# Attention values of the next pair of heads projected beside a pair's first head, values kept per head

## The chip, the core and the metric

The kernel runs on one core of a Trainium2 chip. The metric is the device time of one execution in microseconds (us). Before the change it is 2232.55 us, the median of three runs (2230.82 to 2233.64). The five engines are named as in the profile: PE (TensorE: matmuls; PEld is its weight load), DVE (VectorE), ACT (ScalarE), POOL (GpSimd) and SP (SyncE, whose queue issues the DMAs of the weights).

## What is computed

Two layers of a hybrid block over 256 latent tokens and 256 context tokens, width 1024. The change touches two of the three branches of the token mixing, and of these only how the values are projected:

```python
aq, ak, av, gu, gv, hq, hff, hfb, hi, hg, gates = split_cols(h @ w_in)
...
vals = jnp.concatenate([av.reshape(B, T, ATT_HEADS, ATT_DV), vc], axis=1)
y_att = att_out(diff_attention(q, keys, vals, lam))      # 8 heads of 128 value columns
...
iv = hi.reshape(B, T, HG_HEADS, HG_DV)                   # HGRN2, 8 heads of 128 value columns
_, o_f = hgrn2_scan(k_f, iv, lf_f, s_f, q=qh)
```

Each head needs its own projections: HGRN's forget gates (`w_hff`, both directions), its query and output gate (`w_hqg`), attention's query and key (`w_aqk`). The value matrices, `w_hi` of HGRN and `w_av` of attention, come in blocks of 256 columns, so one block serves a pair of heads (0 and 1, 2 and 3, and so on). All eight heads of a layer work alike; layer 1 computes outputs for the 256 latent tokens only (NQ = 256 instead of 512).

## The kernel before

Each f32 operand is held as two parts, so that a product takes three matmuls (`mm3`, L121 to L123). `load_w` brings a weight block in through SP (two DMAs of 512 KB into `wr`), ACT copies it to `wh` (L111) and DVE subtracts for `wl` (L112). The loads run ahead of the work with high priority; there are three `wr`, four `wh` and four `wl` buffers, a block takes two of each.

The heads stage of a layer goes head by head. While head h's own work runs (`hg_head`: decay levels, scores, state, output; `att_head`: scores, softmax, transposes, values), the projections of head h+1 run on PE. Both are written as Python generators, and `weave` interleaves them: the projections are the main stream, cut into units (one `yield` each: 12 matmuls 512 columns wide, or 24 matmuls 256 wide), and the steps of `hg_head` (13) and `att_head` (11 in layer 0, 7 in layer 1) are spread evenly over 0.92 of the units that `units(h)` counts. PE's instructions stay in the order in which this code issues them. The other engines' order is made by the framework's scheduler when the program is built. All engines work in order.

`project(h)` issues, in layer 0, four units each for `w_hff`, `w_hqg` and `w_aqk` (in layer 1 four, two and three). For an even h it also issues four units for `w_hi` ahead of these and four for `w_av` behind them (`v_proj`, each block 4 units of 24 matmuls). So the weave of an even head (which projects an odd one) has 12 units in layer 0 and 9 in layer 1, and that of an odd head 20 and 17. Head 7 is woven with the next stage's projections (`tail_proj`). `v_proj` copies its two PSUM results to one SBUF tile `v` of 4 x 256 values on ACT (L405); three such tiles rotate.

Three groups of PE instructions carry the argument. Those at L602 (scores of attention) open a head. Those at L626 multiply values by the softmax weights. Those at L321 (`column_sums`) are sums over squares: ACT squares a result (L316), ACT copies its high part (L192), DVE subtracts for the low part (L193, tile `sqs`), then PE sums. L321 runs for attention's norm near the end of a head (just before L534), and for HGRN's norm as its last step (after L543 and L546). The levels' exponents are differences made on DVE (L441, tile `E`) which the scheduler also issues ahead for the next head.

Of the kernel before, what the change touches and what calls it, by code (L numbers as in the profile page):

```python
# [17 lines left out]
P = 128  # L18
# [3 lines left out]
HEADS = 8  # L22
# [25 lines left out]
def trunk(ctx: ExitStack, tc: tile.TileContext, A, out):  # L48
    nc = tc.nc
# [348 lines left out]
    def v_proj(get, src, X, out, name, w=None):  # L398
        if w is None:
            w = load_w(src)  # L400
        v = get("v", [P, 4, 256])
        for tt in range(2):
            ps = PB([P, 2, 256])
            yield from tm_steps(w, X, (2 * tt, 2 * tt + 1), ps)
            nc.scalar.copy(out=v[:, 2 * tt:2 * tt + 2, :], in_=ps)  # L405
        out[name] = v
# [529 lines left out]
    for l in range(DEPTH):  # L936
# [5 lines left out]
        def putter(b, h):  # L942
            return lambda t: nc.sync.dma_start(out=ysp[b, h], in_=t)
# [22 lines left out]
        tc.keep_in_program_order(pre)  # L966
        with pool("heads", lk=2, qg=1, qk=1, v=3, w=2, sq=2, sqs=2 if l else 1, wt=2, sc=1, E=6 if l else 4, K=2, p=2) as get, ExitStack() as even, \
                tc.issue_after(pre.ins):
# [3 lines left out]

            def project(h, out, pss=None):
                if pss is not None:
                    yield from hg_proj(gets[h % 2], l, h, Xh, NQ, out, pss)
                if h % 2 == 0:
                    yield from v_proj(get, A["w_hi"][l, h // 2], Xh, out, "vh", whi if h == 0 else None)
                if pss is None:
                    yield from hg_proj(gets[h % 2], l, h, Xh, NQ, out)
                yield from att_proj(gets[h % 2], l, h, Xh, rope, NQ, out)  # L980
                if h % 2 == 0:
                    yield from v_proj(get, A["w_av"][l, h // 2], Xh, out, "va")

            def units(h):
                return (12 if l == 0 else 9) + (8 if h % 2 == 0 else 0)

            d = {}
            for _ in project(0, d, first):
                pass
            for h in range(HEADS):  # L990
                j = slice((h % 2) * P, (h % 2 + 1) * P)
                m = [hg_head(get, l, h, d["ls"], d["k"], d["qg"][:, 0, :], d["qg"][:, 1, :], d["vh"][:, :, j], putter(1, h),
                             lbv, (reset, masks), NQ),
                     att_head(get, l, d["qk"], d["va"][:, :, j], putter(0, h), attv[l], NQ)]
                if h + 1 < HEADS:
# [216 lines left out]
```

## Time and profile before

| | us |
|---|---|
| median of three runs | 2232.55 |
| the profiled execution's own time | 2240.42 |
| its span, first to last instruction | 2238.6 |
| heads 0 to 5 of layer 0, of the span | 101.11 to 507.85 |
| heads 0 to 5 of layer 1, of the span | 1452.55 to 1763.08 |

The stages are told apart by PE's first matmul at L602 of each head: the window of head h goes from there to the same matmul of head h+1. Such a window holds the units of head h's weave but for the first one or two, and the first one or two of the next weave. The busy time of an engine is what it worked in the window; the rest is idle. PEclk is the granted clock of TensorE as a share of 2.4 GHz; at 0.50 it is 1.2 GHz.

### The profile page before, as it was taken

The page shows a single profiled execution, that of the slowest core. Times are in us where ns is not written, and L with a number is a line of the kernel's source. Part 1 is how long each engine was busy: PE and PEld are TensorE (multiplying, and loading weights), DVE is VectorE, ACT ScalarE, POOL GpSimd, SP SyncE. Part 2 cuts the span into 40 slices and gives each one's busy share as a digit, 9 for nine tenths or more (in the row PEclk, how much of TensorE's full clock was granted, in tenths as well). Part 3 has the DMA queues.
Part 4 walks back from the last instruction along what each step waited for, and adds up shares of the span by engine and source line. Part 5 has one row for each costly group of instructions (what it writes and reads, how often), then busy time and mean ns, then how long its engine had stood idle before and what let it go on. Part 6 is the DMA issues. An engine that isn't in the chain of part 4 may idle for free. (4 is left out here: it accounts for less than half of the span.)

```text
span 2238.6 us, 32836 instructions
## 1 busy us (share of the span) xinstructions
PE 2136.9 (95%) x12448; PEld 1860.9 (83%) x12448; DVE 1713.4 (77%) x2869; ACT 1155.8 (52%) x1920; POOL 315.7 (14%) x272
## 2 busy tenths in 40 slices
PE   8999999999999998989999998999999989997998
PEld 7888788887888886878887877988888879997997
DVE  6799888989767884358776766898899976567786
ACT  3766665656543223245342334666666655455664
POOL 3332132322200000011000002222221210001000
PEclk9999999999999999999999999999999999998999
DMA  7212212212255754344555653322222336654554
GB/s 283 94 67 73 70 66 76 73 65 66 62 174 193 235 161 112 94 159 136 166 187 182 198 148 105 104 91 90 81 90 86 97 99 218 195 183 142 186 194 138
DMA packets 93488, 293.21 MB, mean 131 GB/s; under 512 B 16017, under 2 KB 20753, under 8 KB 93073
## 3 DMA queue, kind: packets, MB, share of 16 engines
q1 hardware_dynamic: 93042, 290.59, 40.1%
q8 instruction: 98, 1.61, 0.3%
q14 instruction: 60, 0.49, 0.1%
q10 hardware_dynamic: 288, 0.52, 0.1%
HBM read 282.66 MB, written 8.41 MB: 130 GB/s over the span
## 5 line engine op out<-in xcount | busy, mean ns | idle before, releaser
L121 PE MATMUL pm<-X,wh 128*128 128x512 f32 (+1 forms) x2032 | 716.1, 352 | 11.0 <-DVE X L255 6.5
L122 PE MATMUL pm<-X,wh 128*128 128x512 f32 (+1 forms) x2032 | 699.0, 344 | 0.0
L123 PE MATMUL pm<-X,wl 128*128 128x512 f32 (+1 forms) x2032 | 698.8, 344 | 0.0
L112 DVE TENSOR_TENSOR wl<-wr,wh 128x1024 fp32r<-128x1024 f32 (+1 forms) x402 | 496.8, 1242 | 203.5 <-ACT wh L111 198.9
L111 ACT CAST wh<-wr 128x1024 fp32r<-128x1024 f32 x408 | 422.0, 1039 | 310.7 <-PE pm L122 172.2
L121 PEld LDWEIGHTS pm<-X,wh 128*128 128x128 f32 x2032 | 386.8, 190 | 61.2 <-DVE X L255 7.9
L123 PEld LDWEIGHTS pm<-X,wl 128*128 128x128 f32 x2032 | 387.1, 190 | 47.3
L122 PEld LDWEIGHTS pm<-X,wh 128*128 128x128 f32 x2032 | 386.5, 190 | 42.1
L225 DVE SCALAR_TENSOR_TENSOR wj<-wa,scr 128x1024 f32<-128x1024 f32 x128 | 156.4, 1222 | 63.4 <-DMA wa<-in_ada_row 60.4
L447 POOL TENSOR_TENSOR K<-qg,E 128x512 f32<-128x512 f32 (+1 forms) x96 | 132.3, 1380 | 461.9 <-PE ps L507 304.3
L121 PE MATMUL pm<-wl,X 128*128 128x256 f32 (+1 forms) x608 | 188.0, 309 | 0.0
L122 PE MATMUL pm<-wh,X 128*128 128x256 f32 (+1 forms) x608 | 183.7, 302 | 0.0
L123 PE MATMUL pm<-wh,X 128*128 128x256 f32 (+1 forms) x608 | 183.7, 302 | 0.0
L202 POOL TENSOR_TENSOR s<-s,mhalf 128x1 f32<-128x1 f32 x26 | 14.3, 550 | 1078.4 <-DVE s L199 1052.7
L121 PE MATMUL pm<-ys,wh 128*128 128x512 f32 (+1 forms) x384 | 129.9, 338 | 10.6 <-ACT wh L111 7.4
L441 DVE TENSOR_TENSOR E<-lk 128x512 f32<-128x512 f32 (+1 forms) x192 | 124.4, 681 | 9.5 <-PE ps L546 8.1
L123 PE MATMUL pm<-ys,wl 128*128 128x512 f32 (+1 forms) x384 | 129.5, 337 | 0.0
L122 PE MATMUL pm<-ys,wh 128*128 128x512 f32 (+1 forms) x384 | 129.5, 337 | 0.0
L121 PEld LDWEIGHTS pm<-wl,X 128*128 128x128 f32 x608 | 117.7, 194 | 6.5 <-issue 2.2
L122 PEld LDWEIGHTS pm<-wh,X 128*128 128x128 f32 x608 | 117.8, 194 | 4.0
L123 PEld LDWEIGHTS pm<-wh,X 128*128 128x128 f32 x608 | 117.4, 193 | 4.2
L442 ACT ACTIVATE E<-E 128x1024 f32<-128x1024 f32 (+1 forms) x96 | 80.9, 846 | 59.9 <-DVE E L441 58.9
(250 smaller groups left out, 3541.3 us busy)
## 6 DMA issues: line engine op xcount, KB each, us to landing
wr<-in_w_up SPq DMA_DIRECT2D x88, 512.0 KB, 4.4
wa<-in_ada_row SPq DMA_DIRECT2D x80, 512.0 KB, 4.1
wr<-in_w_gate SPq DMA_DIRECT2D x48, 512.0 KB, 4.0
wr<-in_w_dn SPq DMA_DIRECT2D x40, 512.0 KB, 4.1
wr<-in_w_hqg SPq DMA_DIRECT2D x32, 512.0 KB, 3.6
wr<-in_w_hff SPq DMA_DIRECT2D x32, 512.0 KB, 3.6
wr<-in_w_aqk SPq DMA_DIRECT2D x32, 512.0 KB, 3.6
wr<-in_w_hi SPq DMA_DIRECT2D x16, 512.0 KB, 4.0
```

The costliest lines, as they stand in the source:

```text
L111: nc.scalar.copy(out=hi, in_=raw)
L112: eng.tensor_tensor(out=lo, in0=raw, in1=hi.bitcast(F32), op=sub)
L121: nc.tensor.matmul(ps, lhsT=lh, rhs=rl, start=first, stop=False)
L122: nc.tensor.matmul(ps, lhsT=lh, rhs=rh, start=False, stop=False)
L123: nc.tensor.matmul(ps, lhsT=ll, rhs=rh, start=False, stop=last)
L202: nc.gpsimd.tensor_tensor(out=r, in0=r, in1=mhalf, op=ALU.pow)
L225: nc.vector.scalar_tensor_tensor(out=junk, in0=raw, scalar=1.0, in1=scr[:, v, :], op0=mul, op1=mul, accum_out=mod[l][:, m, v:v + 1])
L441: nc.vector.tensor_tensor(out=dst, in0=ref if first else src, in1=src if first else ref, op=sub)
L442: nc.scalar.activation(out=E, in_=E, func=AF.Exp)
L447: nc.gpsimd.tensor_tensor(out=mkap(KQ[:], dims, NQ), in0=mkap(q, dims), in1=mkap(E[:], [[2 * b, np_], [b - NQ, 2], [1, b]], NQ), op=mul)
```

## The change

`v_proj` fills two tiles, one per head, of 4 x 128 values, with two copies of 128 x 256 per PSUM result where there was one of 128 x 512; six such tiles rotate. `w_hi` of the next pair stays where it was (beside the second head of a pair, ahead of its units). `w_av` of the next pair moves from the end of the second head's weave to the end of the first head's. `units` counts four units more in the weave of each head but 6 (and 7), so that weaves 0 to 5 have 16 units each in layer 0 and 13 in layer 1.

```diff
     def v_proj(get, src, X, out, name, w=None):
...
-        v = get("v", [P, 4, 256])
+        v = [get("v", [P, 4, P]) for _ in range(2)]
         for tt in range(2):
             ps = PB([P, 2, 256])
             yield from tm_steps(w, X, (2 * tt, 2 * tt + 1), ps)
-            nc.scalar.copy(out=v[:, 2 * tt:2 * tt + 2, :], in_=ps)
+            for i in range(2):
+                nc.scalar.copy(out=v[i][:, 2 * tt:2 * tt + 2, :], in_=ps[:, :, i * P:(i + 1) * P])
         out[name] = v
...
-        with pool("heads", lk=2, qg=1, qk=1, v=3, w=2, sq=2, ...
+        with pool("heads", lk=2, qg=1, qk=1, v=6, w=2, sq=2, ...
...
                 if h % 2 == 0:
-                    yield from v_proj(get, A["w_hi"][l, h // 2], Xh, out, "vh", whi if h == 0 else None)
+                    yield from v_proj(get, A["w_hi"][l, h // 2], Xh, out, ("vh", h // 2), whi if h == 0 else None)
...
-                if h % 2 == 0:
-                    yield from v_proj(get, A["w_av"][l, h // 2], Xh, out, "va")
+                c = 0 if h == 0 else (h + 1) // 2 if h % 2 and h < HEADS - 1 else None
+                if c is not None:
+                    yield from v_proj(get, A["w_av"][l, c], Xh, out, ("va", c))
 
             def units(h):
-                return (12 if l == 0 else 9) + (8 if h % 2 == 0 else 0)
+                return (12 if l == 0 else 9) + (4 if h < HEADS - 1 else 0)
...
-                j = slice((h % 2) * P, (h % 2 + 1) * P)
-                m = [hg_head(get, l, h, d["ls"], d["k"], d["qg"][:, 0, :], d["qg"][:, 1, :], d["vh"][:, :, j], putter(1, h),
+                vh, va = d["vh", h // 2][h % 2], d["va", h // 2][h % 2]
+                m = [hg_head(get, l, h, d["ls"], d["k"], d["qg"][:, 0, :], d["qg"][:, 1, :], vh, putter(1, h),
                              lbv, (reset, masks), NQ),
-                     att_head(get, l, d["qk"], d["va"][:, :, j], putter(0, h), attv[l], NQ)]
+                     att_head(get, l, d["qk"], va, putter(0, h), attv[l], NQ)]
```

SP's queue in layer 0, from the weights of head 1 on, shows the order in which PE uses the blocks. Before:

```order
L110 DMA wr<-in_w_hff 128x1024 x2
L110 DMA wr<-in_w_hqg 128x1024 x2
L110 DMA wr<-in_w_aqk 128x1024 x2
L110 DMA wr<-in_w_hi 128x1024 x2
L110 DMA wr<-in_w_hff 128x1024 x2
L110 DMA wr<-in_w_hqg 128x1024
L943 DMA ysp<-sq 128x512
L110 DMA wr<-in_w_hqg 128x1024
L110 DMA wr<-in_w_aqk 128x1024
L943 DMA ysp<-sq 128x512
L110 DMA wr<-in_w_aqk 128x1024
L110 DMA wr<-in_w_av 128x1024 x2
```

and now:

```order
L110 DMA wr<-in_w_hff 128x1024 x2
L110 DMA wr<-in_w_hqg 128x1024 x2
L110 DMA wr<-in_w_aqk 128x1024 x2
L110 DMA wr<-in_w_av 128x1024 x2
L110 DMA wr<-in_w_hi 128x1024 x2
L110 DMA wr<-in_w_hff 128x1024 x2
L110 DMA wr<-in_w_hqg 128x1024
L944 DMA ysp<-sq 128x512
L110 DMA wr<-in_w_hqg 128x1024
L110 DMA wr<-in_w_aqk 128x1024
L944 DMA ysp<-sq 128x512
L110 DMA wr<-in_w_aqk 128x1024
```

The block `w_av` of heads 2 and 3 now follows head 1's `w_aqk`, and the two value blocks stand next to each other; behind head 2's `w_aqk` the next head's `w_hff` follows at once.

On DVE, what stands ahead of the low part of HGRN's last sum (L193 on `sq`) near the end of a head in layer 1. Before, at the end of head 2 (projecting head 3):

```order
L424 SCALAR_TENSOR_TENSOR lk<-reset,lk 128x512
L425 SCALAR_TENSOR_TENSOR lk<-reset,lk 128x512
L441 TENSOR_TENSOR E<-lk 128x4x64
L112 TENSOR_TENSOR wl<-wr,wh 128x1024
L428 TENSOR_TENSOR w<-lk 128x256
L441 TENSOR_TENSOR E<-lk 128x4x64
L441 TENSOR_TENSOR E<-lk 128x8x32 x2
L441 TENSOR_TENSOR E<-lk 128x16x16
L445 TENSOR_TENSOR K<-lk,E 128x256
L193 TENSOR_TENSOR sqs<-sq,sqs 128x256
```

and now, at the end of head 3 (projecting head 4, `w_aqk` last, as before at the end of head 2):

```order
L425 SCALAR_TENSOR_TENSOR lk<-reset,lk 128x512
L426 SCALAR_TENSOR_TENSOR lk<-reset,lk 128x512
L112 TENSOR_TENSOR wl<-wr,wh 128x1024
L429 TENSOR_TENSOR w<-lk 128x256
L442 TENSOR_TENSOR E<-lk 128x4x64
L193 TENSOR_TENSOR sqs<-sq,sqs 128x256
L442 TENSOR_TENSOR E<-lk 128x4x64
L193 TENSOR_TENSOR sqs<-w,sqs 128x256
```

Of the next head's level work four instructions more (L441 three times, L445) stood ahead of the sum's operand than now (line numbers behind L405 grow by one).

## Rows read from the trace of the kernel before

**Rows 1.** The page's first section: busy us of each engine, share, instructions.

```profile
PE 2136.9 (95%) x12448; PEld 1860.9 (83%) x12448; DVE 1713.4 (77%) x2869; ACT 1155.8 (52%) x1920; POOL 315.7 (14%) x272
```

**Rows 2.** Windows, layer 0, heads 0 to 5: us, busy of PE, PEld, DVE, ACT, POOL, PEclk, DMA.

```profile
101.11:162.17 61.06, 58.19 (x329) 49.05 (x329) 56.15 (x101) 40.02 (x71) 21.93 (x12) 0.97 0.19 66
162.17:235.41 73.24, 72.90 (x449) 63.66 (x448) 60.93 (x104) 44.66 (x77) 16.69 (x12) 1.00 0.23 76
235.41:299.09 63.68, 58.35 (x329) 48.89 (x329) 60.12 (x103) 38.80 (x70) 19.40 (x12) 0.97 0.20 71
299.09:372.31 73.22, 72.91 (x449) 63.67 (x448) 59.91 (x102) 44.67 (x77) 16.60 (x12) 1.00 0.21 69
372.31:434.63 62.32, 58.26 (x329) 48.92 (x329) 58.19 (x102) 39.36 (x71) 23.14 (x12) 0.97 0.21 72
434.63:507.85 73.22, 72.89 (x448) 63.66 (x448) 60.92 (x104) 44.24 (x77) 16.67 (x12) 1.00 0.21 69
```

**Rows 3.** The same for heads 0 to 5 of layer 1.

```profile
1452.55:1493.44 40.89, 37.78 (x261) 33.39 (x260) 39.03 (x80) 27.20 (x55) 10.96 (x12) 1.00 0.32 109
1493.44:1554.25 60.81, 59.92 (x404) 53.56 (x404) 53.11 (x104) 39.44 (x75) 10.88 (x13) 1.00 0.27 83
1554.25:1598.36 44.11, 40.61 (x263) 36.08 (x262) 40.45 (x83) 28.45 (x58) 11.85 (x12) 0.92 0.27 91
1598.36:1659.27 60.91, 60.02 (x406) 53.70 (x406) 53.31 (x104) 39.02 (x74) 10.49 (x12) 1.00 0.26 83
1659.27:1702.17 42.90, 39.38 (x262) 34.87 (x262) 40.87 (x81) 27.73 (x57) 11.41 (x12) 0.96 0.28 93
1702.17:1763.08 60.91, 60.24 (x405) 53.89 (x404) 53.58 (x105) 39.59 (x76) 11.21 (x12) 1.00 0.27 84
```

**Rows 4.** PE's waits, 101.11 to 507.85: us in total, times, longest.

```profile
PE ps L321 <- DVE sqs L193: 4.9, 5, 1.8
PE ps L626 <- DVE sc L465: 3.1, 2, 1.5
```

**Rows 5.** PE's waits, 1452.55 to 1763.08.

```profile
PE ps L321 <- DVE sqs L193: 7.7, 6, 2.7
PE ps L602 <- POOL qk L585: 1.8, 1, 1.8
```

**Rows 6.** Timeline of PE, end of head 2, layer 0: start, us, instruction, idle before.

```profile
280.47 0.72 PE L321 MATMUL ps<-sqs,onesr 128*128 128x512 f32 x2 [1.81 <-DVE sqs L193]
```

**Rows 7.** Timeline of DVE just ahead of that.

```profile
277.43 2.38 DVE L441 TENSOR_TENSOR E<-lk 128x512 f32<-128x512 f32 x2
279.74 0.68 DVE L193 TENSOR_TENSOR sqs<-sq,sqs 128x512 fp32r<-128x512 f32 x1
```

**Rows 8.** Windows of stretches at the lower clock.

```profile
281.52:284.93 3.41, 3.41 (x13) 2.83 (x12) 3.41 (x7) 2.98 (x6) 2.17 (x3) 0.50 0.19 74
1588.82:1595.65 6.83, 6.08 (x28) 6.11 (x29) 6.83 (x17) 3.24 (x7) 2.08 (x3) 0.50 0.17 56
```

**Rows 9.** Timelines of PE and DVE, end of head 2, layer 1.

```profile
1583.73 0.59 PE L121 MATMUL pm<-X,wh 128*128 128x512 f32 x1
1589.57 0.77 PE L321 MATMUL ps<-sqs,onesr 128*128 128x256 f32 x2 [2.69 <-DVE sqs L193]
1585.72 2.50 DVE L441 TENSOR_TENSOR E<-lk 128x256 f32<-128x256 f32 x4
```

**Rows 10.** Groups by line and form, 101.11 to 507.85: count, busy us, mean ns.

```profile
L405 ACT COPY v<-pm 128x512 f32<-128x512 f32 x13 | 7.5, 580 | 9.4 <-PE pm L123 9.4
L621 ACT COPY wt<-ps 128x256 f32<-128x256 f32 x12 | 4.3, 360 | 1.4 <-PE ps L619 1.3
L112 DVE TENSOR_TENSOR wl<-wr,wh 128x1024 fp32r<-128x1024 f32 x50 | 64.4, 1295 | 13.2 <-ACT wh L111 13.1
```

**Rows 11.** Timeline of PE: first and last of 24 matmuls of a value unit.

```profile
1599.25 0.39 PE L121 MATMUL pm<-wl,X 128*128 128x256 f32 x1
1602.07 0.28 PE L123 MATMUL pm<-wh,X 128*128 128x256 f32 x1
```

More of the change, by code (lines that the diff above doesn't have):

```diff
@@ L966, in trunk @@
         tc.keep_in_program_order(pre)
-        with pool("heads", lk=2, qg=1, qk=1, v=3, w=2, sq=2, sqs=2 if l else 1, wt=2, sc=1, E=6 if l else 4, K=2, p=2) as get, ExitStack() as even, \
+        with pool("heads", lk=2, qg=1, qk=1, v=6, w=2, sq=2, sqs=2 if l else 1, wt=2, sc=1, E=6 if l else 4, K=2, p=2) as get, ExitStack() as even, \
                 tc.issue_after(pre.ins):
```

## The prediction, as put on record

> **What bounds the kernel now.** I read the page first: PE is busy 95% of the span [rows 1], so time can come only from stretches where PE stands idle or runs slowly. Then the windows of the heads stages, one row per head. The reader should compare even rows with odd rows. In layer 0 [rows 2], the windows of the odd heads have no idle PE to speak of (73.24 - 72.90 = 0.34 us, then 0.31 and 0.33) while DVE has 12.3, 13.3 and 12.3 us to spare. The windows of the even heads are the reverse: PE idles 2.87, 5.33 and 4.06 us, and DVE is busy 92 to 94% of the window. Layer 1 [rows 3] reads alike: PE idles 3.11, 3.50 and 3.52 us in even windows and 0.89, 0.89 and 0.67 in odd ones; DVE idles 1.9 to 3.7 us in even, 7.3 to 7.7 in odd windows. So two engines take turns as the bound: an even head, woven with few projections, is held by DVE, an odd head by PE. PE idles 13.2 us in the six windows of layer 0 and 12.6 us in those of layer 1, 25.8 in all.
>
> The lists of PE's waits say who is late: mostly DVE, with the low part of a sum's operand (L193 to L321) and the masked score copy ahead of the values (L465 to L626) [rows 4, 5]. The timeline shows how: at 280.47 PE has waited 1.81 us for L193 [rows 6], and L193 had stood behind 2.38 us of level work (L441) [rows 7]. That L441 belongs to the next head; DVE's order puts it ahead.
>
> Behind some of these gaps the granted clock falls. The window from 281.52 to 284.93 is at 0.50, which is 1.2 GHz, right behind the 1.81 us gap; that from 1588.82 to 1595.65 goes with the 2.69 us gap at 1589.57 [rows 8, 9]. In the twelve windows there are three stretches like the first in layer 0 and, in layer 1, the second and one more of 3.41 us. At half the clock the busy part loses half: 4 x 3.41 / 2 + 6.08 / 2 = 9.9 us. With the idle time that makes 35.7 us within reach.
>
> **The move.** One `w_av` block per pair of heads goes from the odd head's weave to the even head's. A value unit of PE takes 24 matmuls; first to last start is 2.82 us [rows 11], 23 steps of 0.123, so 24 of them are 2.9 us and the block 11.8 us. Nothing is saved by that in itself: PE does the same matmuls. With it go two DMAs on SP's queue, two ACT copies and two DVE subtractions of 1.3 us [rows 10]. They stay in the order of use behind `w_aqk`, no load passes another that is needed sooner, and PE's waits inside these windows are at sums, values and scores, the largest of them in [rows 4, 5], and none is for a weight, so I cost these loads at nothing; the cover is the four units of `w_aqk` ahead of them. If it failed, one wait would be about 1.3 us, one late L112.
>
> What the move does is to level the windows. In layer 0, DVE's busy time over what PE needs (its busy time less the 1.7 us lost to the clock) is 174.5 / 169.7 = 1.03 in even windows and 181.8 / 218.7 = 0.83 in odd ones; levelled, it is 356.3 / 388.4 = 0.92 in both. In layer 1 the six windows give 280.4 us of DVE to 297.9 - 4.7 = 293.2 of PE, 0.96. Now if idle time grew in proportion to that share, levelling would change nothing: 0.92 is the mean of both. The gain rests on the curve being bent: at 0.83 PE idles 0.33 us, and it cannot idle less than zero, at 1.03 it idles 4.1. So I go wait by wait.
>
> *Even heads, layer 0.* Their last two steps are now hidden behind value units, which leave no work on DVE, and two units instead of one stand ahead of HGRN's sum; their middle steps have 16 units in place of 12 over which to spread. I take the odd windows' 0.33 plus 0.3 for attention's sum: 0.63 each, 1.9 for three, against 12.3 now.
>
> *Odd heads, layer 0.* These lose something. Between the values (L626) and attention's sum (L321) they had two units; now they have one, of `w_aqk`, as an even head has today. There the wait is between nothing and the 1.8 us of [rows 6]; all waits at L321 in layer 0 make 4.9 us in five [rows 4], 1.0 each. I take 1.0 and add 0.33, and 0.3 for the scores of the next head, which now follow `w_aqk` more closely: 1.6 each, 4.9 for three, against 1.0 now. Layer 0 goes from 13.2 to 6.8: 6.4 us.
>
> *Even heads, layer 1.* Here the wait is HGRN's sum at the head's end, up to 2.69 us [rows 9]. There the operand stood behind four L441 (2.50 us) and one unit of PE, 3.2 us from 1583.73 to where the gap begins, had to hide it. Now a value unit hides it, with DVE's projection work long done. The following head's scores (1.8 us once [rows 5]) also get four units of cover. I take the odd windows' 0.8: 2.4 for three, against 10.1.
>
> *Odd heads, layer 1.* They inherit `w_aqk` at the end, but DVE's order now has only one L441 of the next head ahead of the sum's operand instead of four and a K product. That takes about 2 of the 2.69 us out. I take 0.8 plus 0.6: 1.4 each, 4.2 against 2.5, with bounds of nothing and 2.7 for the sum. Layer 1 goes from 12.6 to 6.6: 6.0 us.
>
> *Clock.* Of six stretches' worth (four of 3.41 us and one of twice that) I let two remain, since some waits of over 1 us stay in odd windows: 9.9 x 4/6 = 6.6 us back. Bounds: nothing and 9.9.
>
> *The split copy.* A copy of 512 values a partition takes 580 ns, and two of 256 take 2 x 360 = 720 [rows 10]. That is 0.14 us for each of 32 results, 4.5 us of ACT in the whole kernel. ACT is busy 52% [rows 1], and behind these copies nothing of the same unit waits: four PSUM buffers rotate and the values are used a head later. Zero, with 4.5 as the upper bound if every one lay on the path. Six half tiles hold what three whole ones did, and the two that a block fills are the ones that the head before has left.
>
> Heads 6 and 7 and all other stages are left as they are.
>
> Sum: 6.4 + 6.0 + 6.6 = 19.0 us off the profiled execution's own 2240.42, 2221.4. The median of the runs is 7.9 us below that execution, so the same step gives 2232.55 - 19.0 = 2213.5.
>
> The Trainium skill, "Perfetto Trace Analysis", section on optimization strategy, says that a kernel whose most contended engine changes over time may gain by interleaving its regimes; this case's trace agrees so far, with DVE busy 92 to 94% of the even and PE over 99% of the odd windows of layer 0. Its section on the most-contended engine warns, however, that matmul busy time is a poor measure of TensorE and weight-load busy time a better one. By that, the result would be another, which stands below as a rival.
>
> **The rivals.**
>
> *The waits only change places.* The odd windows take over the even ones' waits, since they now end with `w_aqk` and start with the next `w_hff` behind them. For it: one unit of cover at L321, in-order DVE. Against it: value units at their start, and 58 us of DVE in 65 of PE instead of 58 in 57. The idle time stays at 25.8, give or take 3: 2229 to 2236.
>
> *Slower: DVE falls behind in every window.* From the odd head's `w_hff` to the even head's `w_aqk` there are now 24 units in a row that each leave work on DVE; the value block that stood in their middle, in which DVE catches up (its 12 to 13 us of idle time in odd windows of layer 0 [rows 2]), is gone. If DVE stays late all through, each of the twelve windows idles as an even one does now: 6 x 4.09 + 6 x 3.38 = 44.8 us against 25.8, 19 us more, 2251.5. It decides from a mean of 35.7 / 12 = 3.0 us lost per window, clock included. Against it: the share of 0.92 is below 1.
>
> *PE had room all along.* If PE's true load is its weight loads, an even window of layer 0 has 61.06 - 49.05 = 12.0 us free [rows 2], which would swallow the 11.8 us block whole, and each odd window would shrink by that: 6 x 11.8 = 71 us, 2162. Against it: a stream of 512-column matmuls without a wait runs in the odd windows with no idle PE, so the weight loads' gaps are no room. The Trainium skill, "Perfetto Trace Analysis", section on the most-contended engine, is what suggests this reading; the trace speaks against it, with 0.3 us of idle PE at 63.7 us of weight loads in 73.2.
>
> *The change does not do what it says*: the copies hold up the PSUM buffers or the halves wait for one another, and the gain is eaten, 2230 to 2235. The order of SP shows that the block does move.
>
> **How the numbers follow.** Chances: the forecast 0.77, the waits change places 0.12, slower 0.08, room in PE 0.01, not as said 0.02. The forecast's own range: at best every window idles as odd ones do now (6 x 0.33 + 6 x 0.82 = 6.9 us) and no clock is lost, 25.8 - 6.9 + 9.9 = 28.8, or 2203.8; at worst the odd windows' bounds are all met (3 x 0.8 more in layer 0, 3 x 2.1 more in layer 1) and half the clock's gain, 3.3, stays out, 19.0 - 2.4 - 6.3 - 3.3 = 7.0, or 2225.6; with the copies' 4.5, 2230. The range of 2203 to 2232 holds that and about half of the rival whose waits change places. A measurement of this kernel can tell about 0.2%, 4.5 us: faster than 2228.1 is 0.76 of the forecast and the 0.01, 0.77; within it 0.01 + 0.10 + 0.02, so 0.13; slower 0.02 + 0.08 = 0.10.
>
> **What would show it.** Right: the windows of heads 0 to 5 become alike (about 66 us each in layer 0, 50 in layer 1), PE's idle time falls to 1 or 2 us in each, DVE's spare time is 5 to 7 us in each of layer 0, no stretch at 0.50 lies in most of them, L321 waits stay at odd heads only. Wrong: idle time of 3 us or more in odd windows, waits at L121 for L112, a wait at L602 at the start of even heads, or ACT's value copies ending PE's waits. Most likely to be mis-sized: L321 in odd heads and the clock.

## The result and the profile after

The changed kernel takes 2262.28 us, the median of four runs (2256.97 to 2265.09), against 2233.1 for the kernel before in the same comparison: a ratio of 1.013 with an interval of 1.0109 to 1.0151. It is slower by 29 us where 19 us less were forecast. The profiled execution took 2263.59, its span is 2261.8, 23.2 more than that of the kernel before (the profiled execution of before lay 7 us over its median, that of after 1 us). Lines of the changed kernel are numbered one higher than before from L405 on: L602 is L603, L441 is L442, L626 is L627 and so on.

The first section of the page reads much as before [rows 1]: PE is busy 2141.4 us and DVE 1724.7. Then the windows of heads 0 to 5 of layer 0, which answer to [rows 2] (length, then busy time of PE, PEld, DVE, ACT and POOL, PEclk, DMA):

```profile
103.39:175.00 71.61, 67.38 (x414) 58.87 (x414) 61.60 (x103) 42.28 (x76) 15.25 (x12) 0.98 0.24 80
175.00:244.22 69.22, 64.92 (x365) 54.41 (x365) 61.31 (x102) 41.74 (x75) 17.56 (x12) 1.00 0.20 67
244.22:315.89 71.67, 67.48 (x413) 58.80 (x413) 60.13 (x102) 42.27 (x75) 15.31 (x12) 0.98 0.20 68
315.89:385.11 69.22, 64.98 (x366) 54.41 (x366) 61.32 (x102) 41.74 (x75) 17.57 (x12) 1.00 0.20 67
385.11:455.13 70.02, 65.83 (x413) 57.31 (x413) 60.69 (x102) 42.27 (x75) 15.32 (x12) 1.00 0.21 71
455.13:523.17 68.04, 62.30 (x354) 52.15 (x354) 60.21 (x101) 41.74 (x75) 17.55 (x12) 1.00 0.19 63
```

The windows did become alike, 68 to 72 us. PE's own work in the six is as before (392.9 us, 393.5 before). But PE now idles about 4.2 us in each of them (71.61 - 67.38, and so on; 5.7 in the last), 26.9 in all against 13.2, and DVE has 8 to 12 us to spare in every one. An even head idles as much as it did on average, and an odd head, which lost 0.33, idles as much as an even one. Layer 1 answers to [rows 3]:

```profile
1467.26:1518.74 51.48, 48.72 (x357) 44.77 (x356) 47.02 (x91) 33.97 (x67) 9.33 (x12) 1.00 0.32 103
1518.74:1569.34 50.60, 48.62 (x310) 42.46 (x309) 41.24 (x76) 29.29 (x59) 8.97 (x11) 1.00 0.27 89
1569.34:1626.72 57.38, 51.21 (x356) 46.65 (x357) 54.24 (x112) 38.61 (x76) 14.48 (x13) 0.97 0.25 83
1626.72:1677.31 50.59, 48.61 (x310) 42.45 (x309) 40.69 (x76) 29.01 (x58) 8.52 (x11) 1.00 0.26 83
1677.31:1735.47 58.16, 53.22 (x356) 48.79 (x356) 54.38 (x113) 38.09 (x76) 14.11 (x13) 0.91 0.26 83
1735.47:1786.05 50.58, 48.63 (x309) 42.46 (x308) 39.51 (x74) 29.02 (x58) 9.16 (x11) 1.00 0.26 82
```

Here the odd heads (second, fourth, sixth row) take 50.6 us with 2.0 idle, but the even heads 2 and 4 take 57.4 and 58.2 with 6.2 and 4.9 idle, and both lose time to the clock as well (PEclk 0.97 and 0.91). The sum over layer 1 is 19.8 us idle against 12.6.

By the lengths, the twelve windows account for 13.0 + 8.3 = 21.3 of the 23.2 us. PE's waits in layer 0, as in [rows 4] (in total, times, longest):

```profile
PE ps L321 <- DVE sqs L193: 9.5, 6, 2.7
PE ps L508 <- DVE sc L466: 7.2, 6, 1.6
PE ps L528 <- DVE E L520: 4.7, 3, 1.6
```

and in layer 1, as in [rows 5]:

```profile
PE ps L321 <- DVE sqs L193: 14.1, 7, 3.9
PE ps L603 <- ACT p L609: 2.4, 2, 1.2
```

In layer 0 the larger waits come back in each head of a kind, to 0.1 us (at attention's sum 2.69, 2.69 and 2.65 us in the even heads): this is no noise, but the order of the instructions. The largest of an even head stands at attention's sum. Its timeline in head 2 of layer 0 (start, us, engine, instruction, idle before), PE first, then ACT, then DVE:

```profile
295.37 1.19 PE L321 MATMUL ps<-sqs,onesr 128*128 128x512 f32 x2 [2.69 <-DVE sqs L193]
```

```profile
291.24 0.63 ACT L192 CAST sqs<-sq 128x512 fp32r<-128x512 f32 x1
```

```profile
291.15 0.87 DVE L456 TENSOR_TENSOR E<-lk 128x512 f32<-128x512 f32 x1
...
291.93 0.47 DVE L578 STREAM_SHUFFLE sh<-pm 128x256 f32<-128x256 f32 x1
292.27 0.42 DVE L579 TENSOR_TENSOR t<-pm,cos 128x256 f32<-128x256 f32 x1
292.59 1.69 DVE L112 TENSOR_TENSOR wl<-wr,wh 128x1024 fp32r<-128x1024 f32 x1
294.20 0.41 DVE L584 TENSOR_TENSOR t<-t,sh 128x256 f32<-128x256 f32 x1
294.54 0.68 DVE L193 TENSOR_TENSOR sqs<-sq,sqs 128x512 fp32r<-128x512 f32 x1
```

ACT had finished the operand of L193 at 291.87. DVE took L193 up at 294.54, 2.67 us later, without a gap in its own work: it did the rest of a level (L456), the rope (rotation by position) of the next head's keys (L578 to L584) and the low part of a weight block (L112), all of which stand ahead of L193 in its order. PE's whole wait of 2.69 us is that queue of work. DVE's 11.5 us of idle time in this window are elsewhere. Cut into six equal parts, the same window shows where:

```profile
244.22:256.17 11.95, 11.84 (x61) 9.11 (x61) 10.91 (x19) 9.33 (x19) 1.63 (x1) 1.00 0.18 69
256.17:268.11 11.94, 11.94 (x71) 10.23 (x71) 11.94 (x26) 8.41 (x15) 3.00 (x2) 1.00 0.13 45
268.11:280.06 11.95, 10.55 (x60) 8.47 (x59) 11.95 (x19) 5.62 (x12) 1.31 (x1) 1.00 0.27 89
280.06:292.00 11.94, 11.94 (x78) 10.68 (x77) 11.31 (x24) 7.98 (x12) 4.95 (x4) 1.00 0.00 0
292.00:303.94 11.94, 9.26 (x53) 8.58 (x52) 8.30 (x14) 4.61 (x9) 4.41 (x4) 0.86 0.32 111
303.94:315.89 11.95, 11.95 (x99) 11.73 (x98) 5.72 (x7) 6.32 (x10) 0.00 (x0) 1.00 0.31 97
```

DVE is full from 256 to 280 and nearly so to 292, and it is busy for only 5.72 of 11.95 us in the last part, where value units now stand. The heads are levelled against one another; a head is not levelled in itself. That alone does not cost the time, though, as e12 will show: there a head is as uneven, and PE hardly waits.

### The profile page after: what moved, and what is told of

It reads as the page before. It is cut to its first block, busy times and chain, and to the rows that moved or that the text cites. A ratio compares the mean times of both kernels' runs of the same rounds, so it can differ in the third digit from the quotient of the medians.

```text
span 2261.8 us, 32865 instructions
## 1 busy us (share of the span) xinstructions
PE 2141.4 (95%) x12448; PEld 1863.5 (82%) x12448; DVE 1724.7 (76%) x2869; ACT 1158.9 (51%) x1952; POOL 292.3 (13%) x272
## 5 line engine op out<-in xcount | busy, mean ns | idle before, releaser
L112 DVE TENSOR_TENSOR wl<-wr,wh 128x1024 fp32r<-128x1024 f32 (+1 forms) x402 | 501.3, 1253 | 211.1 <-ACT wh L111 206.5
L448 POOL TENSOR_TENSOR K<-qg,E 128x512 f32<-128x512 f32 (+1 forms) x96 | 125.1, 1305 | 474.9 <-PE ps L508 308.7
L442 DVE TENSOR_TENSOR E<-lk 128x512 f32<-128x512 f32 (+1 forms) x192 | 113.6, 623 | 11.5 <-PE ps L547 7.5
L443 ACT ACTIVATE E<-E 128x1024 f32<-128x1024 f32 (+1 forms) x96 | 80.9, 846 | 54.4 <-DVE E L442 53.3
```

Source lines behind the costliest of these rows:

```text
L112: eng.tensor_tensor(out=lo, in0=raw, in1=hi.bitcast(F32), op=sub)
L442: nc.vector.tensor_tensor(out=dst, in0=ref if first else src, in1=src if first else ref, op=sub)
L443: nc.scalar.activation(out=E, in_=E, func=AF.Exp)
L448: nc.gpsimd.tensor_tensor(out=mkap(KQ[:], dims, NQ), in0=mkap(q, dims), in1=mkap(E[:], [[2 * b, np_], [b - NQ, 2], [1, b]], NQ), op=mul)
```

## The experiments

Each kernel was run with the kernel before beside it. In the table, idle is PE's idle time in heads 0 to 5 of a layer, from the first scores matmul of head 0 to that of head 6, and the ratio is to the kernel before in the same comparison. The order of layer 0 before the change was profiled four times, three of them with the split copies (before, e1, e6, e9), and idles 13.2, 15.3, 17.3 and 15.0 us: a difference of less than some 4 us between two rows tells nothing.

| kernel | median us | ratio, interval | idle, layer 0 | idle, layer 1 |
|---|---|---|---|---|
| before | 2232.55 | | 13.2 | 12.6 |
| after | 2262.28 | 1.0130, 1.0109 to 1.0151 | 26.9 | 19.8 |
| e1_split_only | 2234.87 | 1.0010, 0.9993 to 1.0027 | 15.3 | 12.9 |
| e2_av_first | 2267.93 | 1.0162, 1.0147 to 1.0178 | 27.2 | 25.1 |
| e3_sums_on_pool | 2277.94 | 1.0211, 1.0185 to 1.0236 | 30.5 | 19.2 |
| e4_hi_even_av_odd | 2244.33 | 1.0050, 1.0033 to 1.0066 | 25.1 | 11.4 |
| e5_empty_step | 2260.11 | 1.0124, 1.0095 to 1.0153 | 26.2 | 20.0 |
| e6_hybrid | 2224.33 | 0.9970, 0.9944 to 0.9995 | 17.3 | 11.6 |
| e7_e4_empty_step | 2244.78 | 1.0053, 1.0036 to 1.0070 | 25.3 | 5.2 |
| e8_before_empty_step | 2262.06 | 1.0131, 1.0104 to 1.0158 | 29.0 | 14.6 |
| e9_hybrid_empty_l1 | 2230.14 | 0.9983, 0.9964 to 1.0001 | 15.0 | 5.5 |
| e10_rate_100 | 2252.88 | 1.0097, 1.0069 to 1.0125 | 13.2 | 20.9 |
| e11_rate_108 | 2269.09 | 1.0160, 1.0133 to 1.0188 | 32.6 | 20.4 |
| e12_level_rate | 2222.74 | 0.9964, 0.9950 to 0.9977 | 10.8 | 5.1 |
| e13_after_no_lo | 2240.35 | 1.0050, 1.0031 to 1.0068 | 17.7 | 12.9 |
| e14_before_no_lo | 2220.35 | 0.9959, 0.9943 to 0.9974 | 14.0 | 8.5 |
| e15_before_rate_100 | 2262.22 | 1.0133, 1.0111 to 1.0156 | 33.5 | 13.3 |
| e16_rate_096 | 2260.13 | 1.0133, 1.0116 to 1.0150 | 26.0 | 19.1 |

### The copies, and where the value blocks stand

**e1_split_only** keeps the half tiles and the two copies and puts `w_av` back where it was.

```diff
-                c = 0 if h == 0 else (h + 1) // 2 if h % 2 and h < HEADS - 1 else None
-                if c is not None:
-                    yield from v_proj(get, A["w_av"][l, c], Xh, out, ("va", c))
+                if h % 2 == 0:
+                    yield from v_proj(get, A["w_av"][l, h // 2], Xh, out, ("va", h // 2))
...
-                return (12 if l == 0 else 9) + (4 if h < HEADS - 1 else 0)
+                return (12 if l == 0 else 9) + (8 if h % 2 == 0 else 0)
```

> The changed kernel with the w_av block put back at the end of the second head's weave (units 12 and 20, as before); the half tiles and the two copies of 256 stay. Theory A (the 24 units in a row that each leave work on DVE are the cause): the waits of before come back, 2233 us, within 5. Theory B (the split copies or the half tiles cost the time): 2245 to 2262. Theory C (attention's and HGRN's sums wait because their low parts, L193, stand behind other work in DVE's order): as A, 2233, since the old spacing of steps comes back too.

1.001 (0.9993 to 1.0027): the copies cost nothing that can be told, at most 0.3%. The loss is the move's.

**e2_av_first** puts the moved block at the start of the even head's weave, so that value units and units that leave work on DVE alternate in blocks.

```diff
+                if h % 2 and h < HEADS - 1:
+                    yield from v_proj(get, A["w_av"][l, (h + 1) // 2], Xh, out, ("va", (h + 1) // 2))
...
-                c = 0 if h == 0 else (h + 1) // 2 if h % 2 and h < HEADS - 1 else None
-                if c is not None:
-                    yield from v_proj(get, A["w_av"][l, c], Xh, out, ("va", c))
+                if h == 0:
+                    yield from v_proj(get, A["w_av"][l, 0], Xh, out, ("va", 0))
```

> The changed kernel with w_av at the start of the even head's weave instead of at its end: 16 and 13 units a weave as now, but each run of 12 units that leave work on DVE is followed by 4 value units. Theory A: PE's idle time in heads 0 to 5 falls from 46.7 us to 25 or less, 2210 to 2238 us. Theory C (sums one unit behind their values, whatever the order of the blocks): both weaves now end with w_aqk, the L321 waits of 23.6 us stay, 2250 to 2265.

**e4_hi_even_av_odd** ends every head with a value block: `w_hi` of the next pair in even heads, `w_av` in odd ones, 16 and 13 units as in the changed kernel.

```diff
-                if h % 2 == 0:
-                    yield from v_proj(get, A["w_hi"][l, h // 2], Xh, out, ("vh", h // 2), whi if h == 0 else None)
+                if h == 0:
+                    yield from v_proj(get, A["w_hi"][l, 0], Xh, out, ("vh", 0), whi)
...
-                c = 0 if h == 0 else (h + 1) // 2 if h % 2 and h < HEADS - 1 else None
-                if c is not None:
-                    yield from v_proj(get, A["w_av"][l, c], Xh, out, ("va", c))
+                if h % 2 == 0:
+                    yield from v_proj(get, A["w_av"][l, h // 2], Xh, out, ("va", h // 2))
+                elif h < HEADS - 1:
+                    yield from v_proj(get, A["w_hi"][l, (h + 1) // 2], Xh, out, ("vh", (h + 1) // 2))
```

> The changed kernel with w_hi of the next pair at the end of the even head's weave and w_av of the next pair at the end of the odd head's: 16 and 13 units a weave, each run of 12 (9) units followed by 4 value units, and every head ends with value units. Theory A: idle time at 25 us or less, 2205 to 2235 us. Theory C: the L321 waits of even heads as now (2.7 us each in layer 0), odd heads like them, 2250 to 2265 us.

Heads 0 to 5 of layer 0 and of layer 1 as one window each, e2 and then e4:

```profile
104.23:520.32 416.09, 388.85 (x2293) 331.63 (x2292) 367.93 (x612) 250.74 (x450) 100.79 (x72) 1.00 0.21 70
1463.76:1793.71 329.95, 304.83 (x1969) 270.92 (x1969) 277.82 (x539) 198.58 (x393) 60.79 (x71) 0.96 0.25 84
```

```profile
104.18:527.58 423.40, 398.29 (x2317) 341.01 (x2316) 360.75 (x611) 253.39 (x451) 92.77 (x72) 0.98 0.20 68
1471.47:1774.73 303.26, 291.85 (x1993) 260.84 (x1993) 279.65 (x556) 204.01 (x402) 68.43 (x72) 1.00 0.28 92
```

In layer 0 these places of the blocks make no difference to the idle time: 416.09 - 388.85 = 27.2 and 423.40 - 398.29 = 25.1 us, 4.2 to 4.5 per head, as after the change. The waits behind it differ. In e2 every head waits as an odd head of the changed kernel does (1.6 us at L508, 1.5 at L528, 0.7 at L620 and 0.5 at attention's sum), in e4 every head waits 2.65 us at attention's sum. In layer 1 the place matters: with a value block at the end of every head (e4) the windows take 303.3 us, 15.5 less than after the change and 7.3 less than before it, and heads 2 and 4, which took 57 to 58 us, take 50; with one at the start of every head (e2) the six take 330. Both times lie outside the ranges of both theories on record; only e4's waits at attention's sum are as one of them had it. Both kernels break the run of 24 units (18 in layer 1) that each leave work on DVE, so breaking it does not bring the time back, in layer 0 in either kernel and in layer 1 in e2. What helps in layer 1 goes with the block at the end of the odd heads, which the even heads follow, and the traces show the waits that go. After the change PE waits in head 2 for 0.6 and 1.2 us at its scores (L603), with the odd head's `w_aqk` just ahead of them, and 3.9 us at HGRN's last sum (L321, behind L547); in e4 it has none of these.

### One wait taken away

**e3_sums_on_pool** lets POOL make the sums' low parts (L193 of `rms_square`), which DVE took up late.

```diff
-    def split(t, src):
+    def split(t, src, eng=nc.vector):
...
-        nc.vector.tensor_tensor(out=t[:, 1, :], in0=src, in1=t[:, 0, :].bitcast(F32), op=sub)
+        eng.tensor_tensor(out=t[:, 1, :], in0=src, in1=t[:, 0, :].bitcast(F32), op=sub)
...
-        return sq, split(get("sqs", [P, 2, n], F32R), sq[:, :n])
+        return sq, split(get("sqs", [P, 2, n], F32R), sq[:, :n], nc.gpsimd)
```

> The changed kernel with the low parts of the two sums of squares per head (L193 on sq) made by POOL instead of DVE, so that they stand behind nothing on DVE. Theory C: the waits at L321, 9.5 + 14.1 us in heads 0 to 5, go for the most part, and the clock with them: 2235 to 2245 us. Theory A: DVE is late in the middle of the run all the same, waits at L508, L528 and L627 stay or grow, and less than half is won: 2248 to 2262 us.

Slower still, 1.0211, and outside both ranges. In this trace POOL takes its L193 up behind an instruction that waits for DVE:

```profile
295.23 0.73 POOL L580 TENSOR_TENSOR sh<-sh,sin 128x256 f32<-128x256 f32 x1 [3.64 <-DVE sh L578]
295.92 2.24 POOL L193 TENSOR_TENSOR sqs<-sq,sqs 128x512 fp32r<-128x512 f32 x1
```

ACT had finished the operand at 294.64, so L193 was 1.28 us late; and it took 2.24 us on POOL, where DVE needs 0.68. PE waits 2.75 us at this sum, where it waited 2.69. So the edit put another queue and a slower instruction in the place of DVE's queue, and it says little about DVE's load.

**e5_empty_step** gives attention's sum more room on PE instead, with one empty step ahead of it; **e8_before_empty_step** does the same to the kernel before.

```diff
         sq = rms_square(get, o, NQ)
-        yield
+        yield; yield
         r = rms_scale(sq, NQ)
...
-                weave(main, n, m, (13, 2 * ns + 3), 0.92 if h + 1 < HEADS else (0.7, 0.85)[l])
+                weave(main, n, m, (13, 2 * ns + 4), 0.92 if h + 1 < HEADS else (0.7, 0.85)[l])
```

> The changed kernel with one empty step of attention's helper between its squares and its sum, and the count of attention's steps raised by one. Attention's sum (L321) then stands two units behind attention's values in layer 0 and three in layer 1, where the changed kernel has one. Theory D (the spacing: one unit is shorter than the way PE, ScalarE, VectorE's queue, PE): the waits of L321 on sqs, 9.5 us in heads 0 to 5 of layer 0 and 14.1 in layer 1, fall below 6 in all, the other waits (L508, L528, L620, some 20) stay, 2240 to 2247 us. Rival (VectorE's own order in levelled heads is late everywhere, so a wait taken from one place comes up at the next): the sum of the waits stays above 35 us, 2255 or more.

> The kernel before with the empty step alone. Theory D: its heads with 12 units have the sum one unit behind the values too, and lose 4.9 us at L321 in layer 0 and 7.7 in layer 1; these shrink to some 3, and 2222 to 2230 us. Rival (a wait removed comes up elsewhere): 2231 to 2236.

In e5 the wait at L321 in layer 0 is gone, as wanted, and one as large stands at the transposes of the softmax weights (L620). The largest of PE's waits in layer 0:

```profile
PE ps L620 <- ACT p L609: 12.2, 6, 2.4
```

The idle time is 26.2 us, 26.9 without the step, and the total is the same. In the kernel before the empty step does harm: 13.2 becomes 29.0 us in layer 0, the total 2262, slower than either theory had it. An empty step costs as much as the whole change. That attention's sum needs only one unit more, and the rest stays, is refuted by both: the empty step gives every later and earlier step of attention another place too.

### The spread of the steps

In `weave`, step i of c stands at (i + 1) / (c + 1) of 0.92 of the units, and waits for the next whole unit. **e10_rate_100**, **e11_rate_108** and **e16_rate_096** change that number for layer 0 of the changed kernel, **e15_before_rate_100** for layer 0 of the kernel before.

```diff
-                weave(main, n, m, (13, 2 * ns + 3), 0.92 if h + 1 < HEADS else (0.7, 0.85)[l])
+                weave(main, n, m, (13, 2 * ns + 3), (0.92 if l else 1.0) if h + 1 < HEADS else (0.7, 0.85)[l])
```

> The changed kernel with layer 0's steps spread over 1.00 instead of 0.92 of a head's units. By the weave's own sum 3 of attention's and 1 of HGRN's steps then stand two units behind the one before, instead of 2 and 0 (the kernel before: 5 and 4 in its heads with 20 units, none in those with 12). Theory F (steps one unit apart wait, and a head with 16 units has hardly more room between steps than one with 12, since a step can only stand at a whole unit): PE's idle per head of layer 0 falls from 4.2 us to some 3.3, 2254 to 2259 us. Rival (the waits sit in VectorE's order and come up elsewhere whatever the spacing): idle of layer 0 stays at 26 to 30 us, 2260 to 2270.

> The same with 1.08: 4 of attention's and 2 of HGRN's steps stand two units behind the one before, and the last ones run into the next head. Theory F: idle per head of layer 0 some 2.1 us, 2246 to 2254 us. Rival: 2260 to 2270, or more, since the last steps of a head then stand directly before the next head's first.

> The changed kernel with layer 0's steps spread over 0.96. Theory F: as at 1.00, idle of layer 0 some 13 us, 2250 to 2256 us. Theory P: another idle time, by the sum one unit behind its values rather the changed kernel's 20 to 27 us, 2257 to 2264.

> The kernel before with layer 0's steps spread over 1.00 of a head's units instead of 0.92. Theory F (room between steps): its heads with 20 units get more room (7 and 5 steps with two units since the one before, instead of 5 and 4), those with 12 none: idle of layer 0 at most 13 us as before, 2228 to 2233 us. Theory P (the place of each step among the others' work, which no count tells): idle of layer 0 above 18 us, 2237 or more.

Heads 0 to 5 of layer 0, e10 and then e15:

```profile
103.81:508.54 404.73, 391.54 (x2317) 333.36 (x2317) 359.71 (x612) 250.37 (x450) 105.87 (x72) 0.99 0.22 72
```

```profile
100.70:530.63 429.93, 396.44 (x2329) 340.24 (x2329) 359.90 (x613) 252.81 (x440) 97.45 (x72) 0.98 0.20 67
```

The same instructions in the changed layout idle 26.9 us at 0.92, 26.0 at 0.96, 13.2 at 1.00 and 32.6 at 1.08. At 1.00 layer 0 takes 404.7 us, 15 less than at 0.92 and 2 less than before the change. The theory of room between steps is refuted by e11, e15 and e16, and e10 gained more than it gave. The count of steps with room ahead of them does not explain the idle time: it is equal at 0.96 and 1.00 and highest at 1.08 (there 3 of HGRN's, if the one past the head's end is counted; the expectation counted 2). And the kernel before goes from 13.2 us at 0.92 to 33.5 at 1.00. Three of its waits at L321, in the heads with 12 units, are now 6.8 us long; they are at HGRN's last sum. So 0.92 suits the old layout; the new one was run at the old one's number.

One wait does follow from a place. In a head of 16 units attention's sum stands one unit behind its values at 0.92 and 0.96 (units 12 and 13), and two behind at 1.00 (12 and 14), at 1.08 (13 and 15) and in e5 (11 and 13). In layer 0 the traces list a wait at this sum in every head with one unit between (0.5 to 2.7 us in the changed kernel, e2 and e4, 2.7 to 3.4 in e16) and in none of e5, e10 and e11. The waits at L321 that e11 still has, 2.1 us in even and 3.4 in odd heads, are at HGRN's last sum, which 1.08 puts past the head's last unit. The whole idle time does not follow: e5 and e11 lose as much elsewhere.

### How much is DVE's load

**e13_after_no_lo** and **e14_before_no_lo** leave out the subtraction that makes the low part of the heads' weights (L112); the matmul that uses it takes the high part, so the outputs are not those of the kernel. PE's order stays, 116 DVE instructions go.

```diff
-        lo = wp.tile([P, 1024 // w, w], F32R, tag="wl", name="wl", bufs=4)[:, :k1 - k0, :]
+        lo = hi if eng is None else wp.tile([P, 1024 // w, w], F32R, tag="wl", name="wl", bufs=4)[:, :k1 - k0, :]
...
-        eng.tensor_tensor(out=lo, in0=raw, in1=hi.bitcast(F32), op=sub)
+        eng is None or eng.tensor_tensor(out=lo, in0=raw, in1=hi.bitcast(F32), op=sub)
```

> The changed kernel; VectorE's subtraction that makes the low part of the weights (L112) is left out in the heads' projections of both layers, and the matmul that would use it takes the high part: PE's work and order as in the changed kernel, VectorE has 117 instructions of 1.2 to 2.3 us less. The outputs lack the weights' low parts. Theory G (VectorE's queue makes the steps late): PE's idle in heads 0 to 5 of layer 0 falls from 26.9 to 10 us or less and in layer 1 from 19.8 to 8 or less: 2230 to 2240 us. Rival H (the step's own way is longer than a unit): idle stays at 20 or more in layer 0, 2250 to 2262.

> The same left out of the kernel before. Theory G: its heads with 12 units lose most of their idle time too, from 13.2 us in layer 0 to 5 or less, 2215 to 2225 us, and the gap to the changed kernel shrinks from 29 to 10 to 20 us. Rival H: idle 11 to 13 us, 2228 to 2233, the gap stays at 25 to 30.

Layer 0, heads 0 to 5, e13 and e14:

```profile
104.35:513.87 409.52, 391.85 (x2317) 337.04 (x2317) 303.75 (x562) 251.42 (x450) 88.39 (x72) 0.98 0.21 69
```

```profile
101.71:508.55 406.84, 392.87 (x2331) 336.03 (x2330) 301.36 (x562) 250.36 (x438) 93.42 (x72) 0.99 0.21 70
```

Of the theory that DVE's queue makes the steps late, the times came out (2220.35 inside its range, 2240.35 at the edge of it, a gap of 20 us), but not the idle times. DVE's 365 us became 304, and the changed kernel's idle time in layer 0 fell from 26.9 to 17.7, while the kernel before stayed at 14.0. The gap between the two kernels shrank from 29 to 20 us by the medians, from 21.3 to 10.8 us by the lengths of the twelve windows and from 20.9 to 8.1 us by PE's idle time in them. So a sixth to a fifth of DVE's work makes between a third and three fifths of the loss; what the rest of it makes, these two runs do not tell. The largest wait left in e13, 3.51 us at L321 in odd heads, shows one way in which it goes on. PE had done attention's values at 351.9; ACT was free to square them, but it took an exponent of the levels first, and that waited for DVE:

```profile
353.14 1.06 ACT L443 ACTIVATE E<-E 128x1024 f32<-128x1024 f32 x1 [3.46 <-DVE E L442]
354.11 0.62 ACT L458 ACTIVATE E<-E 128x512 f32<-128x512 f32 x1
354.63 1.03 ACT L111 CAST wh<-wr 128x1024 fp32r<-128x1024 f32 x1
355.56 0.59 ACT L316 ACTIVATE sq<-ps 128x512 f32<-128x512 f32 x1
```

The squares (L316) start 3.7 us after the values were there: 1.2 us of that is the wait for DVE, and 2.4 is ACT's own work ahead of them. An engine with idle time to spare is late when the first instruction in its order waits.

### What beats both

**e7_e4_empty_step** is e4 with the empty step. **e6_hybrid** has layer 0 as before and layer 1 as e4; **e9_hybrid_empty_l1** is e6 with the empty step in layer 1. **e12_level_rate** is e4 with the number 1.00 in heads 0 to 5 of layer 0 and the empty step in layer 1:

```diff
         sq = rms_square(get, o, NQ)
         yield
+        if l:
+            yield
...
-                weave(main, n, m, (13, 2 * ns + 3), 0.92 if h + 1 < HEADS else (0.7, 0.85)[l])
+                weave(main, n, m, (13, 2 * ns + 3 + l), (1.0 if l == 0 and h < 6 else 0.92) if h + 1 < HEADS else (0.7, 0.85)[l])
```

> The layout with HGRN's values at the end of even heads and attention's at the end of odd ones in both layers (e4, 2244.33 us), and the empty step ahead of attention's sum. Theory D: L321's 2.65 us per head of layer 0 go, six to seven times, and layer 1 stays: 2225 to 2231 us. Rival (waits come up at the next step): 2240 to 2247.

> Layer 0 in the layout before (units 12 and 20, both value projections beside the odd head), layer 1 with HGRN's values of the next pair at the end of an even head and attention's at the end of an odd one (units 13 and 13). Theory D: layer 0 takes 406 us for heads 0 to 5 as before and layer 1 some 303 to 305 instead of 310.5: 2225 to 2228 us. Rival (the 7 us of layer 1 were the clock's luck and not the layout): 2231 to 2235.

> Layer 0 in the layout before (units 12 and 20, no empty step), layer 1 with HGRN's values at the end of even heads and attention's at the end of odd ones and with the empty step ahead of attention's sum. Theory E (each layer's idle time depends on its own placement alone, and a placement is good or bad by which step stands one unit behind what it needs): layer 0's heads 0 to 5 take 406 us as in the hybrid without the step, layer 1's 296 as in e7, 9 less than that hybrid: 2214 to 2219 us. Rival (the layers' times drift with each other or with the clock): 2222 or more.

> Levelled in both layers with HGRN's values at the end of even heads and attention's at the end of odd ones; layer 0 with the spread 1.00 up to head 5 and 0.92 at head 6, layer 1 with 0.92 and the empty step ahead of attention's sum. If a layout's idle time follows from where its steps stand alone: layer 0 takes 6 x 67.1 = 403 us for heads 0 to 5 (the changed kernel at 1.00 had 67.1 in the heads that end alike), layer 1 296 as in e7: 2216 to 2222 us. Rival (the gain at 1.00 hung on the other place of the values): 2228 or more.

e7 did nothing in layer 0 (25.3 us idle) and much in layer 1 (5.2, where e4 had 11.4), by the same step; its total is in the rival's range. e6 came out 0.7 us below its range, with the windows as expected (406.6 and 305.3 us). e9 did not: its profiled windows in layer 1 are 7 us shorter than e6's, its median is not, and the interval holds 1. Its trace shows the gain being lost behind them: from head 6 of layer 1 to the end it takes 483.4 us against 469.0 in e6. A wait of 3.3 us at the first scores of head 7 (L603, for POOL's L586), which e6 does not have, is part of it, and the granted clock of the 40 us behind it is 0.87 against 0.96; e7 and e12 have the same wait. e12 in layer 0 and layer 1:

```profile
103.60:503.25 399.65, 388.82 (x2317) 330.42 (x2316) 356.64 (x611) 250.63 (x450) 108.73 (x72) 1.00 0.21 72
1443.95:1740.23 296.28, 291.15 (x1981) 259.43 (x1980) 269.94 (x553) 204.90 (x401) 64.86 (x72) 1.00 0.28 91
```

Both layers are levelled here, with 16 and 13 units per head, and idle 10.8 and 5.1 us. The kernel takes 2222.74 against 2230.75 for the kernel before, 0.9964 (0.9950 to 0.9977), 0.7 us above its range: the fastest of those that compute the whole, though not to be told from e6 (0.9970). The windows are 21.3 us shorter than those of the profile before, the median 8.0; of the difference, 8.3 is that the profiled execution of before lay 9.7 over this comparison's median and that of e12 1.4 over its own, and the other stages give up 5.0. So levelled heads need not cost time. Nor need an uneven head: parts two to four of six of e12's head 2 in layer 0 show DVE full for 33 us, longer than after the change, and PE idles 1.6 us in the whole head.

```profile
248.50:259.64 11.14, 11.14 (x68) 9.41 (x67) 11.14 (x25) 8.23 (x16) 3.03 (x2) 1.00 0.14 48
259.64:270.79 11.15, 11.15 (x64) 9.47 (x63) 11.15 (x21) 6.32 (x12) 3.44 (x1) 1.00 0.29 96
270.79:281.93 11.14, 11.14 (x76) 10.15 (x75) 11.14 (x19) 4.82 (x8) 5.63 (x4) 1.00 0.14 47
```

## Why the prediction was wrong

**The bound.** Right: PE is the bound, and the time lost is PE's idle time; the slower kernels have more of it and the same PE work. That two engines take turns was right as an average over a window. The step that failed is the next one: that with a levelled share of 0.92 only the waits beside the moved block have to be priced, which gave 0.63 us of idle time to an even and 1.6 to an odd head of layer 0, and 0.8 to an even head of layer 1. The move gives every step of a weave another place, and what PE waits for is where a step's operand stands in the order of ACT's or DVE's work. The share itself is not at fault: at the same share the changed kernel idles 13.2 us in layer 0 in place of 26.9 once its steps are spread over 1.00 (e10). Even there it does not reach the 6.8 that were forecast.

**Even heads, layer 0**: predicted 0.63 us each, measured 4.2. The reason given for the head's end came true, since HGRN's last sum no longer waits there; but it had made only 1.1 us of the 12.3. And "their middle steps have 16 units in place of 12 over which to spread" failed. At 0.92, a head with 16 units sets eleven attention steps at units 2, 3, 4, 5, 7, 8, 9, 10, 12, 13, 14, still one unit apart but for two; a head with 20 has five such gaps. Attention's sum came to stand one unit behind its values, at a place where DVE had 2.67 us of other work ahead of its operand.

**Odd heads, layer 0**: predicted 1.6 each, measured 4.2 to 5.7. The one unit of cover at L321 was seen and priced at 1.0; it costs 0.5. What was not seen are the other steps, which moved as well: L508 waits 1.6 for the merged scores and L528 up to 1.6 for the state. I costed only the waits whose neighbours in the code had changed, but `units` moves every step of every head.

**Layer 1**: odd heads predicted 1.4, measured 2.0. Even heads predicted 0.8, measured 2.8, 6.2 and 4.9. The largest wait is the one at HGRN's last sum, which a value unit was to hide: the unit stands there, and PE still waits 3.9 us in head 2 (PE, then ACT):

```profile
1619.11 0.50 PE L321 MATMUL ps<-sqs,onesr 128*128 128x256 f32 x2 [3.90 <-DVE sqs L193]
```

```profile
1617.10 0.37 ACT L316 ACTIVATE sq<-ps 128x256 f32<-128x256 f32 x1
```

PE had ended HGRN's output at 1612.4; ACT squared it only at 1617.10, behind exponents of the levels (L443) that had waited 1.5 and 1.0 us for DVE. With a value block at the end of the odd head ahead as well, in e4, heads 2 and 4 take 50 us and this wait is gone. I had looked at a head's own units and not at those of the head before.

**Clock**: two of six stretches' worth were to remain. By PEclk, two of layer 0's windows still lose 0.02, and two of layer 1's 0.03 and 0.09 of their length, some 10 us in all, as much as before. Nothing came back.

**The split copy**: predicted at nothing, and e1 shows nothing.

**The other stages**: predicted unchanged; they make 1.9 us together.

**The rivals.** The slower one gave 44.8 us of idle time and 2251.5; measured were 26.9 + 19.8 = 46.7 and 2262. Its idle time was right, but by luck: its mechanism is the run without a value block, and e2, which breaks the run, idles 52.3 us. It had a chance of 0.08. The evidence against it was the share of 0.92, the same mean that the main sum leaned on. The rival in which waits change places was right in kind (e5 shows it bare) but took their sum as fixed. That PE had room all along is out, since its busy time stayed as it was; that the change does not do what it says is out by e1 and by the windows, which did become alike.

**What stays open.** The waits shown here were followed to the queue that made them, the others were not. That attention's sum does not wait when two units stand between is read off several runs; the idle time of a whole layout, and so why 1.00 suits the levelled one and 0.92 the old one, follows from no count that was tried. A simulation of all queues in their order, with durations from the trace, might tell it; that was not made. Nor was the order of DVE or ACT changed by itself.

## What to carry to other kernels

A window's mean busy share does not tell what a step waits for, and neither does the share in a part of it: for each wait, compare the end of the operand's producer with the start of its consumer, to see whether the producer's work was late or the consumer's queue. In a woven order, a block that is moved resets the place of every step, so price all waits of a head again and not only those beside the edit. Numbers like the 0.92 belong to the layout that they were found with: compare two layouts each at a number of its own, before calling one slower.

## What the hardware showed that I had not expected

A DVE instruction can take several times as long while POOL works. A copy of 128 x 4 values (L474) takes 1.25 us in all six heads of layer 0 after the change and 0.16 before it (there L473), where POOL is idle at those times:

```profile
L474 DVE COPY s<-E x6: 1252/1257/1259, 122.0 to 469.3; 128x4 f32<-128x4 f32 x6
```

```profile
L473 DVE COPY s<-E x6: 153/161/163, 125.8 to 449.6; 128x4 f32<-128x4 f32 x6
```

In head 0 it starts inside a POOL product and ends with it (POOL, then DVE):

```profile
121.50 1.70 POOL L448 TENSOR_TENSOR K<-qg,E 128x512 f32<-128x512 f32 x1 [3.14 <-DVE s L607]
```

```profile
121.98 1.25 DVE L474 COPY s<-E 128x4 f32<-128x4 f32 x1
```

The Trainium skill, "SBUF — State Buffer", section on SBUF's two separate sides, says that GpSimd and certain DVE instructions (in a two-port mode, or with two SBUF inputs) share one pair of ports, that the one which starts first holds it for its whole instruction, and that the other is blocked meanwhile. The trace agrees: 121.98 + 1.25 = 123.23, and POOL's product ends at 123.20; all six copies end 0.03 us behind a POOL product in this way. DVE's busy time in heads 0 to 5 of layer 0 went from 356.2 us before [rows 2] to 365.3 after, for the same work; how much of that is POOL's doing is not shown.
